# Planner of the RWKV recurrence stage: priority of the modulation rows, length of the small inverse's steps, gap before Tm's second group of matmuls

## Chip, cores and metric

The kernel runs on one NeuronCore of a Trainium2 chip. The metric is the device time of one execution in microseconds (us), the median of several runs. Engines are named as in the profile: PE (matmuls), DVE (vector engine), ACT (scalar engine), POOL (GpSimd, here almost only an issuer of DMAs) and SP (issuer of DMAs). Every engine works through its own queue in order, and waits for other engines through semaphores.

## The reference

One decoder block over 512 tokens with 2048 channels, all in float32. `c` gives six modulation vectors (shift, scale and gate for two sub-layers). The first sub-layer projects the modulated, RMS-normalised input once and feeds two mixers: RWKV-7 (a recurrence with a 64 x 64 state for each of 16 heads) and causal pooling. The second is a gated MLP.

```python
mod = silu(c) @ w_ada + b_ada                       # 6 * 2048
h = rmsnorm(x, g1) * (1 + sc1) + sh1
p = h @ w_in                                        # r, k, v, three small ranks, pool inputs
def step(S, inp):                                   # the recurrence, over 512 tokens
    sa = einsum('bhvk,bhk->bhv', S, a_t)
    S = S * w_t + sa * b_t + v_t * k_t
    y = einsum('bhvk,bhk->bhv', S, r_t)
y_pool[g] = (causal mean of u over (2, 4, 8, 16)[g] - u) @ pool_w[g]
x = x + gt1 * (concat(y_rwkv, y_pool) @ w_out)
h = rmsnorm(x, g2) * (1 + sc2) + sh2
x = x + gt2 * ((silu(gate) * val) @ w_down)         # gate, val: causal conv of h @ w_up
```

## The kernel before

The kernel has five stages in a row: the first eight column tiles of the input projection; the **recurrence stage**, which holds the other 27 column tiles beside the recurrence; the output projection; the up-projection; the down-projection. Only the recurrence stage is touched by the change.

In the recurrence stage activations lie channel by token, 128 x 512. Every float32 product is made of three fp32r matmuls (high and low halves, line 547), so the 27 tiles of `projection` are 27 x 48 = 1296 matmuls of 512 columns. Their weights come in 108 blocks: `weights` lets ACT round a block to its high half (516) and DVE subtract the low half (523), and ACT issues a later block's load. A block feeds 12 matmuls. The heads are worked off in eight pairs. For each pair `stage_a` makes decays and keys, scores, and the inverse of eight 64 x 64 unit triangular matrices; `stage_b` does the state. The inverse starts with 16 x 16 blocks: POOL carries them through DRAM into a layout with one block to a partition (lines 755, 759), DVE solves 14 steps of one multiply (769) and one add (771) each, in place (`xyl`), and POOL carries the result back (777, 781). `stage_b` then joins 16 to 32: 32 small matmuls into `pT` (886), a masked copy on DVE into `Tm` (890), 48 more matmuls which read `Tm` (896, 900), additions on DVE (903, 906); next 32 to 64 (914 to 933), the solves (940, 952 to 959), and a scan over the eight chunks in which six PE matmuls (980) alternate with six DVE steps (982). `post` normalises and gates the pair's output (1002 to 1023), and POOL stores it (1026).

Beside this, `ada_rows` makes three of the six modulation vectors, which are wanted only after the stage: 48 x 4 = 192 **modulation rows**, each a 256 KB load on SP (640) into one of five buffers and one DVE instruction with a sum (658) over it; four quarters, each with its own part `cq` of the activated `c` (635), which has one buffer.

The order of all this is not written out. Each chain is a Python generator that yields its next operation: engine, length, earliest time. `run` keeps a clock for each engine, and always takes the operation that can start first; on one engine it prefers one with a smaller priority number if that could start within 0.3 us of the first. The instructions are recorded in the order taken, and the chip keeps that order on each engine. The lengths are constants in the code; nothing at run time corrects them. Priorities: opening and evictions 0, `all_b` 1, `all_a` 2, weights 0 to 4 by how far ahead they are, `stage_k` 3, pool groups 5, projection 6, modulation rows 7. Row n is due from 3.0 + n * SPAN / 192 on, which is one row every 2.4 of the planner's microseconds; SPAN is 460 and a row's planned length ADAB is 0.72.

Of the kernel before, what the change touches and what calls it, by code (L numbers as in the profile page):

```python
# [9 lines left out]
F32 = mybir.dt.float32  # L10
# [6 lines left out]
P = 128  # L17
# [12 lines left out]
NA = 4  # L30
# [5 lines left out]
SPAN = 460.0  # L36
# [29 lines left out]
def block_kernel(ctx, tc, a, out, stop=None, dbg=None):  # L66
    nc = tc.nc
    V, S, G, PE = nc.vector, nc.scalar, nc.gpsimd, nc.tensor
# [126 lines left out]
    free_at = {"P": 0.0, "V": 0.0, "S": 0.0, "Q": 0.0, "G": 0.0}  # L195

    def spawn(prio, gen):
        chains.append([prio, gen, next(gen)])
# [188 lines left out]
    ra = actx.enter_context(tc.tile_pool(name="ra", bufs=1))  # L387
# [46 lines left out]
    def jl(j):  # L434
        return slice(j * L, (j + 1) * L)

    def rktile(name):
        return ra.tile([P, T], F32, tag="rk", name=name, bufs=3)

    def vtile(name):  # L440
        return ra.tile([P, T], F32, tag="v", name=name, bufs=2)

    def rpad(name):
        return ra.tile([P, 16 + T], F32, tag="rpad", name=name, bufs=4)
# [11 lines left out]
    modq = ra.tile([P, NA, 48], F32, tag="modq", name="modq")  # L456

    def load_lw(p):
        qs[p].lw = ra.tile([P, P], F32, tag="lw", name="lw")
        nc.sync.dma_start(qs[p].lw, a["lora"][p, :, 0, :])  # L460

    def load_pw(gi):
# [86 lines left out]
                cur[0] += 1  # L549
            spawn(0, evict(ti, ps, tag, t))  # L550

    upads = {}

    def evict(ti, ps, tag, t):
        if ti < 21:
            p, i = ti // 3 + 1, ti % 3
            q = qs[p]
            dst = vtile("v") if i == 2 else rktile("rk")
            t = yield "S", 0.6, t
            shift1(ps, 8 * i + p, dst)  # L560
            t = yield "V", 0.65, t
            shift2(ps, 8 * i + p, dst)
            mm.give(tag, t)
            if i == 0:
                q.rk = []
            if i < 2:
                q.rk.append((dst, t))
            else:
                q.v, q.made = (dst, t), t
        else:  # L570
            n, i = divmod(ti - 21, 2)
            gi = (1, 2, 0)[n]
            u = rpad("upad")
            V.memset(u[:, 0:16], 0.0)
            t = yield "S", 0.5, t
            S.copy(u[:, 16:], ps)
            mm.give(tag, t)
            if i == 0:
                upads[gi] = [load_pw(gi), u]
            elif gi:  # L580
                spawn(5, pool_group(gi, upads[gi][0], [upads[gi][1], u], t))
            else:
                upads[gi].append(u)

    def pool_front(gi, upad, t):
        win = WINS[gi]
        zs = []
        for i in range(2):
            cur_, lo, step = upad[i], 1, 1
            while step < win:  # L590
                t = yield "V", 0.64, t
                nxt = rpad("sw")
                V.tensor_add(nxt[:, lo:], cur_[:, lo:], cur_[:, lo - step : 16 + T - step])
                cur_ = nxt
                step *= 2
                lo += step
            z = upad[i][:, 16:]
            t = yield "V", 1.0, t
            edge = ra.tile([P, 16], F32, tag="edge", name="edge")
            V.tensor_mul(edge[:, 0:win], cur_[:, 16 : 16 + win], prec[:, 0:win])  # L600
            V.tensor_sub(edge[:, 0:win], edge[:, 0:win], z[:, 0:win])
            V.scalar_tensor_tensor(z, cur_[:, 16:], 1.0 / win, z, op0=ALU.mult, op1=ALU.subtract)
            V.tensor_copy(z[:, 0:win], edge[:, 0:win])
            zs.append(z)
        return zs, t
# [17 lines left out]

    def pool_group(gi, pw, upad, t):
        zs, t = yield from pool_front(gi, upad, t)
        yield from pool_back(gi, zs, pw, t + 2.0)

    last_mix = []
# [9 lines left out]
    def load_ada(n):  # L638
        t = ra.tile([P, AT], F32, tag="war", name="war", bufs=WARB)
        nc.sync.dma_start(t, a["ada2"][n // 48, n % 48, :, :])  # L640
        was.append(t)

    def ada_rows():
        n_all = 48 * NA
        step = SPAN / n_all
        t = yield "Q", 0.35, 1.0
        load_cq(0)
        tcq = t + 5.0
        land = {}
        for n in range(WARB - 1):  # L650
            t = yield "Q", 0.35, 0.0
            load_ada(n)
            land[n] = t + 6.0
        for n in range(n_all):
            kq, j = divmod(n, 48)
            t = yield "V", ADAB, max(land[n], tcq, 3.0 + n * step)
            wa = was.pop(0)
            V.scalar_tensor_tensor(wa, wa, 1.0, cqs[kq], op0=ALU.mult, op1=ALU.mult, accum_out=modq[:, kq, j : j + 1])
            if j == 47 and kq < NA - 1:
                tq = yield "Q", 0.35, t  # L660
                load_cq(kq + 1)
                tcq = tq + 5.0
            if n + WARB - 1 < n_all:
                tq = yield "Q", 0.35, 0.0
                load_ada(n + WARB - 1)
                land[n + WARB - 1] = tq + 6.0

    def stage_a(p, q):
        yield "-", 0.0, have(q, "made")
        (r, tr), (k, tk), (v, tv) = q.rk[0], q.rk[1], q.v  # L670
        lw = q.lw
# [91 lines left out]
        prod = ra.tile([64, 56], F32, tag="prod", name="prod")  # L763
        for s in range(1, 15):
            n = 15 - s
            t = yield "V", 0.36, t
            pv = prod[:, 0 : s * n].rearrange("p (j t) -> p j t", j=s)
            yv = xyl[:, 1, 0:s, s + 1 : 16]
            V.tensor_tensor(pv, xyl[:, 1, 0:s, s : s + 1].to_broadcast([64, s, n]),
                            nl[:, s : s + 1, s + 1 : 16].to_broadcast([64, s, n]), op=ALU.mult)  # L770
            V.tensor_add(yv, yv, pv)
            t -= 0.2
# [12 lines left out]
    def stage_k(p, q, t):  # L785
        (r, tr), (k, tk), (v, tv) = q.rk[0], q.rk[1], q.v
        al, em = q.al, q.em
        t = yield "S", 0.72, t
        S.activation(al, al, AF.Identity, bias=drv[:, 27 + p : 28 + p], scale=col("ka", p))
        t = yield "V", 0.63, t  # L790
        V.tensor_mul(k, k, al)
        kt = q.kt = ra.tile([P, T], F32, tag="kt", name="kt", bufs=2)
        t1 = yield "V", 0.63, t
        V.tensor_mul(ch(kt), ch(k), em[:, :, 1 : L + 1])
        q.tkt = t1
        t = yield "V", 0.68, t
        V.scalar_tensor_tensor(k, r, col("rk", p), k, op0=ALU.mult, op1=ALU.mult)
        t = yield "P", 1.1, pa.when(t)
        psb, tag = pa.take()
        PE.matmul(psb, bones, k, start=True, stop=True)  # L800
        bv = q.bv = ra.tile([P, T], F32, tag="bv", name="bv", bufs=2)
        t = yield "V", 0.63, t
        V.tensor_mul(bv, psb, v)
        pa.give(tag, t)
# [14 lines left out]
    def stage_b(p, q):  # L819
# [69 lines left out]
        t = yield "V", 0.36, t  # L889
        V.tensor_mul(Tm, r32(pT), mlev[:, None, :].to_broadcast([P, 8, 32]))  # L890
        pa.give(tag, t)
        t = yield "P", 1.0, max(t, tpb)
        pX = btile()[:, 0, :]
        for s in range(8):
            for b in range(4):
# [132 lines left out]
    def all_a():  # L1028
        for p in range(NP):
            yield from stage_a(p, qs[p])  # L1030

    def all_b():
        for p in range(NP):
            yield from stage_b(p, qs[p])
# [13 lines left out]
    pa.free.clear()  # L1048

    with tc.manual_schedule():  # L1050
        for prio, gen in ((0, opening()), (1, all_b()), (2, all_a()), (weights_prio, weights()), (6, projection()), (7, ada_rows())):
            spawn(prio, gen)
        run()

# [618 lines left out]
```

## Time and profile before

| | us |
|---|---|
| median of 3 runs | 2265.96 |
| lowest, highest | 2261.97, 2266.63 |
| profiled execution, its own time | 2266.95 |
| its span, first to last instruction | 2264.8 |
| lines 547, first to last (recurrence stage) | 140.6 to 688.1 |

The profile is of one execution. Times inside it are counted from the start of the span. "Idle before, releaser" is the time for which an engine stood still before an instruction, and what ended it. PEclk is the TensorE clock that the chip granted, 1.00 being full speed. A wait is put down to the dependency that came last.

### The profile page before, as it was taken

The numbers are of one execution on the slowest core, as the hardware profiler recorded it, in microseconds if no ns is written. First come the engines' busy times: TensorE is split into PE (matmuls) and PEld (weight loads), VectorE is DVE, ScalarE is ACT, GpSimd is POOL, SyncE is SP. The second block draws the span as 40 slices with busy tenths as digits, with TensorE's granted clock in tenths as the row PEclk, the third lists the DMA queues.
The fourth block names the chain that finished last, engine by engine and source line by source line (L and its number), as shares of the span: only waits on it lengthen the run. The fifth ranks groups of instructions, "written<-read, shape, count | busy, mean of one in ns | idle before, by whom it ended". The sixth has DMA issues, their size and how long they took to land.

```text
span 2264.8 us, 42575 instructions
## 1 busy us (share of the span) xinstructions
PE 2178.5 (96%) x17060; PEld 1908.8 (84%) x17060; DVE 1622.9 (72%) x2546; ACT 1019.7 (45%) x1465; POOL 217.8 (10%) x352
## 2 busy tenths in 40 slices
PE   6899989999999999999999999999999999999997
PEld 3666767677677889999999999999999888888886
DVE  7998878888764578888888877777777455353465
ACT  4353434343334356555555555555556322233453
POOL 0011111111010001100100000000000000110000
PEclk9999999999999999999999999999999999999999
DMA  9946566655537665988888877777777577663464
GB/s 395 374 165 188 174 186 181 174 159 149 176 113 248 190 196 186 287 239 244 234 237 245 220 199 198 194 196 203 198 198 218 180 264 262 209 205 114 131 191 155
DMA packets 169992, 468.64 MB, mean 207 GB/s; under 512 B 21361, under 2 KB 29505, under 8 KB 161729
## 3 DMA queue, kind: packets, MB, share of 16 engines
q1 hardware_dynamic: 128866, 364.45, 48.1%
q0 software_dynamic: 24752, 72.91, 15.5%
q10 hardware_dynamic: 16176, 28.58, 4.6%
q8 instruction: 133, 2.18, 0.4%
q14 instruction: 65, 0.53, 0.1%
HBM read 433.86 MB, written 31.99 MB: 206 GB/s over the span
## 4 chain that ended last, share of the span: by engine, by line
PE 70%; DVE 2%; DMA 1%; ACT 1%; issue 0%; DVEq 0%; ACTq 0%
PE b L133 18%; PE b L131 18%; PE b L132 18%; PE b L1110 5%; PE b L1111 3%; PE mm L547 2%; PE pa L612 0%; DMA wrow<-wup 0%; ACT x L1193 0%; DMA wraw<-wout 0%; PE mm L132 0%; PE mm L133 0%; PE py L133 0%; PE pa L133 0%; PE pa L132 0%
## 5 line engine op out<-in xcount | busy, mean ns | idle before, releaser
L133 PE MATMUL b<-t,ulo 128*128 128x256 f32 x1408 | 397.2, 282 | 0.0
L131 PE MATMUL b<-t,uhi 128*128 128x256 f32 x1408 | 396.8, 282 | 0.0
L132 PE MATMUL b<-t,uhi 128*128 128x256 f32 x1408 | 396.7, 282 | 0.0
L131 PE MATMUL b<-y,uhi 128*128 128x256 f32 x1056 | 298.2, 282 | 1.3 <-ACT uhi L1260 1.3
L133 PE MATMUL b<-y,ulo 128*128 128x256 f32 x1056 | 297.9, 282 | 0.3 <-DVE ulo L1262 0.3
L132 PE MATMUL b<-y,uhi 128*128 128x256 f32 x1056 | 297.8, 282 | 0.0
L547 PE MATMUL mm<-ahl,whi 128*128 128x512 f32 x864 | 294.5, 411 | 0.0
L1262 DVE TENSOR_TENSOR ulo<-wd,uhi 128x1024 fp32r<-128x1024 f32 (+1 forms) x120 | 136.0, 1134 | 207.7 <-ACT uhi L1260 198.7
L131 PEld LDWEIGHTS b<-t,uhi 128*128 128x128 f32 x1408 | 266.9, 190 | 0.0
L133 PEld LDWEIGHTS b<-t,ulo 128*128 128x128 f32 x1408 | 266.9, 190 | 0.0
L132 PEld LDWEIGHTS b<-t,uhi 128*128 128x128 f32 x1408 | 266.8, 190 | 0.0
L1260 ACT CAST uhi<-wquart 128x1024 fp32r<-128x1024 f32 x156 | 163.8, 1050 | 203.8 <-PE b L132 178.6
L1260 ACT CAST uhi<-wd 128x1024 fp32r<-128x1024 f32 (+1 forms) x120 | 117.3, 978 | 282.3 <-PE b L132 231.2
L1262 DVE TENSOR_TENSOR ulo<-wquart,uhi 128x1024 fp32r<-128x1024 f32 x156 | 190.7, 1223 | 71.4 <-ACT uhi L1260 71.3
L1260 ACT CAST uhi<-r 128x1024 fp32r<-128x1024 f32 x132 | 138.6, 1050 | 163.3 <-PE b L132 158.5
L133 PE MATMUL b<-act,ulo 128*128 128x512 f32 x528 | 208.7, 395 | 0.0
L131 PE MATMUL b<-act,uhi 128*128 128x512 f32 x528 | 208.1, 394 | 0.0
L132 PE MATMUL b<-act,uhi 128*128 128x512 f32 x528 | 208.1, 394 | 0.0
L1262 DVE TENSOR_TENSOR ulo<-r,uhi 128x1024 fp32r<-128x1024 f32 x132 | 161.2, 1221 | 62.6 <-ACT uhi L1260 62.6
L131 PEld LDWEIGHTS b<-y,uhi 128*128 128x128 f32 x1056 | 200.3, 190 | 1.8 <-ACT uhi L1260 1.7
L133 PEld LDWEIGHTS b<-y,ulo 128*128 128x128 f32 x1056 | 200.1, 190 | 0.7 <-DVE ulo L1262 0.7
L132 PEld LDWEIGHTS b<-y,uhi 128*128 128x128 f32 x1056 | 199.9, 189 | 0.1
(312 smaller groups left out, 4310.7 us busy)
## 6 DMA issues: line engine op xcount, KB each, us to landing
wquart<-wup SPq DMA_DIRECT2D x176, 512.0 KB, 4.8
wa<-ada SPq DMA_DIRECT2D x48, 1024.0 KB, 6.8
war<-ada SPq DMA_DIRECT2D x192, 256.0 KB, 4.5
wd<-wdn SPq DMA_DIRECT2D x80, 512.0 KB, 4.1
wraw<-win ACTq DMA_DIRECT2D x105, 256.0 KB, 4.1
wraw<-wout SPq DMA_DIRECT2D x96, 256.0 KB, 3.6
wquart<-wup POOLq DMA_DIRECT2D x44, 512.0 KB, 7.4
r<-wup SPq DMA_DIRECT2D x44, 512.0 KB, 4.5
```

The costliest lines, as they stand in the source:

```text
L131: PE.matmul(ps, wh, xh, start=start, stop=False, skip_group_check=more)
L132: PE.matmul(ps, wh, xl, start=False, stop=False, skip_group_check=more)
L133: return PE.matmul(ps, wl, xh, start=False, stop=stop, skip_group_check=more)
L547: PE.matmul(ps, w[:, sl], x, start=first, stop=k == KT - 1 and i == 2)
L1110: PE.matmul(ps[:, :].rearrange("p (a b) -> p a b", a=2), wh, x, start=start, stop=False)
L1111: PE.matmul(ps[:, 0:HT], wl, x[:, 0, :], start=False, stop=stop)
L1260: S.copy(hi[:, 0:n], src)
L1262: lo_of[0] = V.tensor_tensor(lo[:, 0:n], src, hi[:, 0:n].bitcast(F32), op=ALU.subtract)
```

## The change

All of it is in the planner's rules for the recurrence stage.

- **Rows.** The fixed priority 7 of `ada_rows` becomes `rows_prio`: 0 while DVE's planned clock is past the due time of the row three after the next one, else 7. A quarter's `cq` is taken to land 7 instead of 5 after its issue.
- **Small inverse.** A step (one multiply and one add) is planned at 0.46 instead of 0.36; the next one may still start 0.2 earlier.
- **Gap.** The second group of matmuls of the 16-to-32 join (896) may be planned no earlier than 3.0 after `Tm`.
- **Buffers.** The evictions of r and k wait, in the plan, for one of the three `rk` buffers (`rk_free`); before, only the chip waited. The loads `lw` get a second buffer. The copies of pool inputs wait for the pool group before (`pooling`).

No computing instruction is added or removed on any engine.

```diff
--- before.py
+++ after.py
@@ -434,7 +434,15 @@
     def jl(j):
         return slice(j * L, (j + 1) * L)
 
+    rk_made, rk_left = [0], []
+
+    def rk_free(t):
+
+        n = rk_made[0] - 3
+        return t if n < 0 else max(t, rk_left[n]) if n < len(rk_left) else None
+
     def rktile(name):
+        rk_made[0] += 1
         return ra.tile([P, T], F32, tag="rk", name=name, bufs=3)
 
     def vtile(name):
@@ -456,7 +464,7 @@
     modq = ra.tile([P, NA, 48], F32, tag="modq", name="modq")
 
     def load_lw(p):
-        qs[p].lw = ra.tile([P, P], F32, tag="lw", name="lw")
+        qs[p].lw = ra.tile([P, P], F32, tag="lw", name="lw", bufs=2)
         nc.sync.dma_start(qs[p].lw, a["lora"][p, :, 0, :])
 
     def load_pw(gi):
@@ -549,14 +557,14 @@
                 cur[0] += 1
             spawn(0, evict(ti, ps, tag, t))
 
-    upads = {}
+    upads, pooling = {}, [0.0]
 
     def evict(ti, ps, tag, t):
         if ti < 21:
             p, i = ti // 3 + 1, ti % 3
             q = qs[p]
+            t = yield "S", 0.6, t if i == 2 else (lambda t=t: rk_free(t))
             dst = vtile("v") if i == 2 else rktile("rk")
-            t = yield "S", 0.6, t
             shift1(ps, 8 * i + p, dst)
             t = yield "V", 0.65, t
             shift2(ps, 8 * i + p, dst)
@@ -570,14 +578,15 @@
         else:
             n, i = divmod(ti - 21, 2)
             gi = (1, 2, 0)[n]
+            t = yield "S", 0.5, (lambda t=t: None if pooling[0] is None else max(t, pooling[0]))
             u = rpad("upad")
             V.memset(u[:, 0:16], 0.0)
-            t = yield "S", 0.5, t
             S.copy(u[:, 16:], ps)
             mm.give(tag, t)
             if i == 0:
                 upads[gi] = [load_pw(gi), u]
             elif gi:
+                pooling[0] = None
                 spawn(5, pool_group(gi, upads[gi][0], [upads[gi][1], u], t))
             else:
                 upads[gi].append(u)
@@ -623,6 +632,7 @@
 
     def pool_group(gi, pw, upad, t):
         zs, t = yield from pool_front(gi, upad, t)
+        pooling[0] = t
         yield from pool_back(gi, zs, pw, t + 2.0)
 
     last_mix = []
@@ -639,13 +649,18 @@
         t = ra.tile([P, AT], F32, tag="war", name="war", bufs=WARB)
         nc.sync.dma_start(t, a["ada2"][n // 48, n % 48, :, :])
         was.append(t)
+
+    done_rows = [0]
+
+    def rows_prio():
+        return 0 if free_at["V"] > 3.0 + (done_rows[0] + 3) * SPAN / (48 * NA) else 7
 
     def ada_rows():
         n_all = 48 * NA
         step = SPAN / n_all
         t = yield "Q", 0.35, 1.0
         load_cq(0)
-        tcq = t + 5.0
+        tcq = t + 7.0
         land = {}
         for n in range(WARB - 1):
             t = yield "Q", 0.35, 0.0
@@ -654,12 +669,13 @@
         for n in range(n_all):
             kq, j = divmod(n, 48)
             t = yield "V", ADAB, max(land[n], tcq, 3.0 + n * step)
+            done_rows[0] = n + 1
             wa = was.pop(0)
             V.scalar_tensor_tensor(wa, wa, 1.0, cqs[kq], op0=ALU.mult, op1=ALU.mult, accum_out=modq[:, kq, j : j + 1])
             if j == 47 and kq < NA - 1:
                 tq = yield "Q", 0.35, t
                 load_cq(kq + 1)
-                tcq = tq + 5.0
+                tcq = tq + 7.0
             if n + WARB - 1 < n_all:
                 tq = yield "Q", 0.35, 0.0
                 load_ada(n + WARB - 1)
@@ -763,7 +779,7 @@
         prod = ra.tile([64, 56], F32, tag="prod", name="prod")
         for s in range(1, 15):
             n = 15 - s
-            t = yield "V", 0.36, t
+            t = yield "V", 0.46, t
             pv = prod[:, 0 : s * n].rearrange("p (j t) -> p j t", j=s)
             yv = xyl[:, 1, 0:s, s + 1 : 16]
             V.tensor_tensor(pv, xyl[:, 1, 0:s, s : s + 1].to_broadcast([64, s, n]),
@@ -798,6 +814,7 @@
         t = yield "P", 1.1, pa.when(t)
         psb, tag = pa.take()
         PE.matmul(psb, bones, k, start=True, stop=True)
+        rk_left.extend((t, t))
         bv = q.bv = ra.tile([P, T], F32, tag="bv", name="bv", bufs=2)
         t = yield "V", 0.63, t
         V.tensor_mul(bv, psb, v)
@@ -889,7 +906,7 @@
         t = yield "V", 0.36, t
         V.tensor_mul(Tm, r32(pT), mlev[:, None, :].to_broadcast([P, 8, 32]))
         pa.give(tag, t)
-        t = yield "P", 1.0, max(t, tpb)
+        t = yield "P", 1.0, max(t, tpb) + 3.0
         pX = btile()[:, 0, :]
         for s in range(8):
             for b in range(4):
@@ -1048,7 +1065,7 @@
     pa.free.clear()
 
     with tc.manual_schedule():
-        for prio, gen in ((0, opening()), (1, all_b()), (2, all_a()), (weights_prio, weights()), (6, projection()), (7, ada_rows())):
+        for prio, gen in ((0, opening()), (1, all_b()), (2, all_a()), (weights_prio, weights()), (6, projection()), (rows_prio, ada_rows())):
             spawn(prio, gen)
         run()
 
```

The lists that follow are instructions in the order recorded for one engine. In the new kernel lines after 434 have higher numbers: 523 is 531, 547 is 555, 658 is 674, 769 and 771 are 785 and 787, 886 is 903, 890 is 907, 896 is 913, 900 is 917, 982 is 999.

**PE, third head pair, between the two groups of the 16-to-32 join.** `x` holds the 16 x 16 inverses, `sb` the score matrices, `mm` the projection. Before:

```order
L886 MATMUL pa<-x_2713,sb 32x32 x32
L547 MATMUL mm<-ahl,whi 128x512
L547 MATMUL mm<-ahl,wlo 128x512
L547 MATMUL mm<-ahl,whi 128x512 x2
L547 MATMUL mm<-ahl,wlo 128x512
L547 MATMUL mm<-ahl,whi 128x512
L896 MATMUL pb<-x_2713,Tm_3164 32x32 x32
L900 MATMUL pb<-Tm_3164,x_2713 32x32 x16
```

With the change:

```order
L903 MATMUL pa<-x_2881,sb 32x32 x32
L726 MATMUL pa<-sq,hmat 128x512
L555 MATMUL mm<-ahl,wlo 128x512
L555 MATMUL mm<-ahl,whi 128x512 x2
L555 MATMUL mm<-ahl,wlo 128x512
L555 MATMUL mm<-ahl,whi 128x512 x2
L555 MATMUL mm<-ahl,wlo 128x512
L555 MATMUL mm<-ahl,whi 128x512 x2
L555 MATMUL mm<-ahl,wlo 128x512
L555 MATMUL mm<-ahl,whi 128x512 x2
L913 MATMUL pb<-x_2881,Tm_3359 32x32 x32
L917 MATMUL pb<-Tm_3359,x_2881 32x32 x16
```

Between the groups stood 6 projection matmuls; now 12, and the key norm's matmul of the next pair (line 726, formerly 710).

**DVE, third head pair, ahead of the copy into Tm.** `war` are modulation rows, `wlo` low halves of weight blocks, `cs` the decay sums of the next pair. Before:

```order
L658 SCALAR_TENSOR_TENSOR war,modq<-war,cq 128x512 x4
L450 SCALAR_TENSOR_TENSOR rk<-mm,vec,rk 128x511
L523 TENSOR_TENSOR wlo<-wraw,whi 128x512
L658 SCALAR_TENSOR_TENSOR war,modq<-war,cq 128x512 x2
L523 TENSOR_TENSOR wlo<-wraw,whi 128x512
L658 SCALAR_TENSOR_TENSOR war,modq<-war,cq 128x512 x4
L523 TENSOR_TENSOR wlo<-wraw,whi 128x512
L658 SCALAR_TENSOR_TENSOR war,modq<-war,cq 128x512 x2
L523 TENSOR_TENSOR wlo<-wraw,whi 128x512
L658 SCALAR_TENSOR_TENSOR war,modq<-war,cq 128x512 x2
L450 SCALAR_TENSOR_TENSOR v<-mm,vec,v 128x511
L890 TENSOR_TENSOR Tm_3164<-pa,mlev 128x256
```

With the change:

```order
L674 SCALAR_TENSOR_TENSOR war,modq<-war,cq 128x512 x5
L531 TENSOR_TENSOR wlo<-wraw,whi 128x512
L674 SCALAR_TENSOR_TENSOR war,modq<-war,cq 128x512
L531 TENSOR_TENSOR wlo<-wraw,whi 128x512
L674 SCALAR_TENSOR_TENSOR war,modq<-war,cq 128x512
L712 SCALAR_TENSOR_TENSOR cs<-scanm,sg 128x520
L716 COPY mid<-cs 128x8
L717 TENSOR_TENSOR cs<-cs,mid 128x520
L674 SCALAR_TENSOR_TENSOR war,modq<-war,cq 128x512
L531 TENSOR_TENSOR wlo<-wraw,whi 128x512
L907 TENSOR_TENSOR Tm_3359<-pa,mlev 128x256
```

Rows in runs of two and four, up to the copy, became rows that mostly stand alone; a run of five is left further up. Over the whole stage 36 rows stood alone on DVE and the longest run was seven; now 141 stand alone and the longest run is five.

**DVE, the scan of the third head pair.** `rw` is the state that the scan runs through, `xyl` and `prod` the small inverse of the pair after it. Before:

```order
L982 SCALAR_TENSOR_TENSOR rw<-pb,fdec,rw 128x64
L726 TENSOR_TENSOR bt<-sq,al 128x512
L982 SCALAR_TENSOR_TENSOR rw<-pb,fdec,rw 128x64
L728 TENSOR_TENSOR bt<-bt,em 128x512
L982 SCALAR_TENSOR_TENSOR rw<-pb,fdec,rw 128x64
L735 SCALAR_TENSOR_TENSOR ar<-sq,ep 128x512
L982 SCALAR_TENSOR_TENSOR rw<-pb,fdec,rw 128x64
L450 SCALAR_TENSOR_TENSOR rk<-mm,vec,rk 128x511
L982 SCALAR_TENSOR_TENSOR rw<-pb,fdec,rw 128x64
L737 TENSOR_TENSOR ar<-rk,ep 128x512
L982 SCALAR_TENSOR_TENSOR rw<-pb,fdec,rw 128x64
```

With the change:

```order
L999 SCALAR_TENSOR_TENSOR rw<-pb,fdec,rw 128x64
L778 TENSOR_TENSOR xyl<-nl,lanei 64x256
L785 TENSOR_TENSOR prod<-xyl,nl 64x14
L787 TENSOR_TENSOR xyl<-xyl,prod 64x14
L999 SCALAR_TENSOR_TENSOR rw<-pb,fdec,rw 128x64
L674 SCALAR_TENSOR_TENSOR war,modq<-war,cq 128x512
L999 SCALAR_TENSOR_TENSOR rw<-pb,fdec,rw 128x64
L785 TENSOR_TENSOR prod<-xyl,nl 64x26
L787 TENSOR_TENSOR xyl<-xyl,prod 64x2x13
L785 TENSOR_TENSOR prod<-xyl,nl 64x36
L787 TENSOR_TENSOR xyl<-xyl,prod 64x3x12
L999 SCALAR_TENSOR_TENSOR rw<-pb,fdec,rw 128x64
```

Between scan steps stood preparations of the next pair; now these stand ahead of the scan, and single rows and the small inverse of the next pair, from its first instruction on (778, formerly 762), stand there. So it is in the scans of the first and of the third to the seventh pair. On PE the stage's pairs end later: behind the last pair's last matmul (1012, now 1029) stood 73 of the 1296 projection matmuls, and now 15.

## The prediction

> **What bounds the kernel now.** I began with the busy time by stage, in five stretches that cover the recurrence stage. The columns are PE, PEld, DVE, ACT and POOL busy (instructions), the granted clock, DMA share and GB/s.
>
> ```profile
> 140.00:260.00 120.00, 111.95 (x1103) 84.26 (x1101) 101.46 (x259) 52.49 (x84) 22.84 (x42) 0.97 0.62 184
> 260.00:380.00 120.00, 111.59 (x1446) 85.85 (x1447) 99.61 (x260) 46.01 (x76) 21.69 (x40) 0.96 0.57 169
> 380.00:500.00 120.00, 112.62 (x1462) 85.69 (x1461) 98.68 (x255) 48.70 (x79) 18.36 (x34) 0.97 0.57 165
> 500.00:640.00 140.00, 129.19 (x1525) 97.15 (x1527) 111.23 (x294) 51.66 (x85) 25.05 (x47) 0.94 0.58 168
> 640.00:700.00 60.00, 59.95 (x599) 46.56 (x589) 33.94 (x71) 22.53 (x39) 2.17 (x4) 1.00 0.42 124
> ```
>
> PE sets the pace: it is busy for 525.3 of 560 us, and stands for 34.7. DVE is the second engine (444.9 of 560, 79%). The clock is below 1.00 in four of the five rows; that matters further down. The stage can gain no more than PE's idle time, plus what the reduced clock cost. So the next view is who PE waited for in the stage (us in total, times, longest).
>
> ```profile
> PE pb L896 <- DVE Tm L890: 16.6, 6, 4.9
> PE mm L547 <- DVE wlo L523: 6.2, 3, 4.2
> ```
>
> Half of PE's idle time is one wait, that of the join's second group for the copy into `Tm`, in six of eight pairs. The same view for DVE shows why so short a copy is late:
>
> ```profile
> DVE war L658 <- DMA war<-ada: 33.9, 34, 2.5
> DVE war L658 <- DMA cq<-cact: 5.2, 2, 2.6
> ```
>
> DVE stood for 39.1 us in front of modulation rows whose data had not landed, and what is behind them in its queue waits too. The third pair in the timeline, PE first, then DVE (start, length, what, idle before it and releaser):
>
> ```profile
> 315.04 0.75 PE L886 MATMUL pa<-x,sb 32*32 32x32 f32 x64
> ...
> 322.23 1.08 PE L896 MATMUL pb<-x,Tm 32*32 32x32 f32 x64 [4.85 <-DVE Tm L890]
> 323.11 1.05 PE L900 MATMUL pb<-Tm,x 32*32 32x32 f32 x32
> 324.08 1.22 PE L679 MATMUL pa<-xwa,lw 64*128 64x512 f32 x1
> ```
> ```profile
> 320.49 0.69 DVE L658 SCALAR_TENSOR_TENSOR war<-war,cq 128x512 f32<-128x512 f32 x1 [1.09 <-DMA war<-ada]
> ...
> 321.76 0.41 DVE L890 TENSOR_TENSOR Tm<-pa,mlev 128x256 f32<-128x256 f32 x1
> ```
>
> The first group ended at 315.79; the copy began at 321.76, behind a pile of rows, the last of which waited 1.09 us for its load. Six projection matmuls were too little cover.
>
> The reduced clock belongs to these gaps. These are the only stretches of the stage in which the clock was halved:
>
> ```profile
> 189.00:195.80 6.80, 4.50 (x11) 3.53 (x12) 6.29 (x19) 0.62 (x1) 2.44 (x5) 0.50 0.46 106
> 322.10:332.40 10.30, 10.17 (x145) 6.55 (x145) 5.80 (x14) 4.17 (x7) 0.00 (x0) 0.50 0.43 143
> 445.00:451.80 6.80, 4.95 (x102) 2.79 (x102) 4.26 (x12) 1.90 (x2) 0.00 (x0) 0.50 0.60 187
> 513.30:520.10 6.80, 5.02 (x104) 4.28 (x105) 6.12 (x14) 1.67 (x3) 0.00 (x0) 0.50 0.54 177
> 574.70:585.00 10.30, 9.70 (x143) 6.53 (x143) 5.66 (x15) 3.74 (x7) 0.00 (x0) 0.50 0.54 164
> ```
>
> Each begins at the end of one of the five longest PE gaps. Four are waits for `Tm`, the one above among them; the first is the wait for a weight block at 191.30, quoted below. Shorter gaps had no such effect: from 258 to 300 the clock stayed at 1.00 although PE stood for 1.59 us.
>
> ```profile
> 258.00:300.00 42.00, 38.10 (x584) 28.81 (x584) 36.87 (x97) 19.53 (x32) 4.72 (x9) 1.00 0.51 151
> 260.56 1.07 PE L886 MATMUL pa<-x,sb 32*32 32x32 f32 x64 [1.59 <-issue]
> ```
>
> **The change, part by part.** No instruction comes or goes, so the sum consists of waits alone. It is made against the profiled execution, 2266.95, which is 1.0 above the median.
>
> **Rows and gap: the wait for Tm, -16.** Now 12 or more projection matmuls stand between the groups in seven pairs, eight in the last, instead of 0 to 6. Two of them take 0.46 us, from start to start:
>
> ```profile
> 309.96 0.61 PE L547 MATMUL mm<-ahl,whi 128*128 128x512 f32 x2
> 310.42 0.39 PE L547 MATMUL mm<-ahl,wlo 128*128 128x512 f32 x1
> ```
>
> So 12 cover 2.8 us. That alone would leave part of the long waits, for the copy came 6.0 us after the first group in the example. But its lateness was the pile of rows, and with rows standing alone the four loads in flight have some 2.4 us of plan time for each row. Ahead of the copy remain about a row, a weight block and the copy, 0.69 + 0.69 + 0.41 = 1.8 us, under 2.8. Bounds: 16.6 if all goes, about 8 if the gap helps and the pile does not thin; I take 16. The longer gap costs nothing as long as projection matmuls fill it. Without that cover it is 3.0 us in eight pairs, 24 us; the recorded order has matmuls there in every pair.
>
> **Small inverse at its measured length: the wait for weight blocks, -4.** The 4.2 us of the second row of PE's waits fall into the first pair:
>
> ```profile
> 181.72 0.69 DVE L523 TENSOR_TENSOR wlo<-wraw,whi 128x512 fp32r<-128x512 f32 x1
> ...
> 190.57 1.88 DVE L523 TENSOR_TENSOR wlo<-wraw,whi 128x512 fp32r<-128x512 f32 x3
> 191.30 0.79 PE L547 MATMUL mm<-ahl,wlo 128*128 128x512 f32 x1 [4.24 <-DVE wlo L523]
> 185.19 0.20 DVE L769 TENSOR_TENSOR prod<-xyl,nl 64x44 f32<-64x44 f32 x1
> 185.65 0.21 DVE L769 TENSOR_TENSOR prod<-xyl,nl 64x50 f32<-64x50 f32 x1
> ```
>
> A step takes 0.46 us (185.19 to 185.65), and the plan of 0.36 loses 1.4 us over 14 steps. DVE made no low half for 8.9 us and PE ran dry. In the new order 14 blocks stand ahead of this inverse on DVE instead of 11, which is 36 matmuls or 8.2 us more cover. Bounds 0 and 6.2; I take 4, since the two other waits (2.0 in sum) have other places.
>
> **The clock, -13.** Take away the five long gaps and the halved stretches should go with them. In these PE was busy for 34.3 us (the five rows added up). From the start of 896 to what follows 900, the third pair took 322.23 to 324.08, 1.85 us; the fourth, at full clock, 1.17:
>
> ```profile
> 389.14 0.72 PE L896 MATMUL pb<-x,Tm 32*32 32x32 f32 x62 [0.59 <-DVE Tm L890]
> ...
> 390.31 0.73 PE L547 MATMUL mm<-ahl,whi 128*128 128x512 f32 x2
> ```
>
> At that ratio, 1.58, the 34.3 us would have been 21.7, a gain of 12.6; were all work twice as slow, 17.2. I take 13, near the measured ratio. [...]
>
> **What the new order costs, +8.** First the scan, +3. In six scans the small inverse's first instruction (762) now stands between scan steps. If its data (`nl`, which POOL carries through DRAM) is late, DVE holds up the scan, and PE's next 980 behind it. The data was there 11.2 us after the masked scores (746) in one pair and 14.6 in another:
>
> ```profile
> 349.83 1.28 DVE L746 TENSOR_TENSOR sb<-pa,masks 128x512 f32<-128x512 f32 x2
> 362.32 0.42 DVE L762 TENSOR_TENSOR xyl<-nl,lanei 64x256 f32<-64x256 f32 x1 [0.19 <-DMA nl<-dn]
> 472.07 1.28 DVE L746 TENSOR_TENSOR sb<-pa,masks 128x512 f32<-128x512 f32 x2
> 487.92 0.42 DVE L762 TENSOR_TENSOR xyl<-nl,lanei 64x256 f32<-64x256 f32 x1 [3.55 <-DMA nl<-dn]
> ```
>
> Bounds 0 and 6 x 3.55 = 21; of eight such steps two waited before, one of them long, so I take one or two long waits, less the 1 us of matmuls between scan steps: 3. Second the tail, +2: 15 projection matmuls (3.4 us) instead of 73 (16.6) follow the last pair's PE work, but the output projection needs that pair only at its end, and its first mixes now stand on DVE between the last scan steps; bounds 0 and 5. Third, +3 for waits that I cannot place: DVE does the same work in less time (444.9 in about 535, 83%). The second `lw` buffer, the later `cq` and the waits for `rk` and pools move waits that the plan did not know into it; PE's rows above show none of them, so they count 0.
>
> Sum: -16 - 4 - 13 + 3 + 2 + 3 = -25, and 2266.95 - 25 = **2242**.
>
> **Rivals.** **Late inverse stops the scans (slower).** The place is 762 between scan steps in six pairs. Before, it waited by 3.55 at most, once. From about 4 us on, PE's idle time there passes 3.0 (after 1 us of matmuls), the length of the shortest gap that had a halved clock; then each costs 3.1 of idle time and 13 / 5 = 2.6 of clock, six of them 34. Against the other terms (-28) that gives 2273. For it: POOL's descriptors share the DMA engines with rows now spread evenly. Against it: one long wait in eight, and 3.55 is short of 4. **The clock does not come back.** PE still halves, through several short gaps in a row or new long ones elsewhere: without the 13, 2255. For it: DVE at 83% with a strict order. Against it: the 258 to 300 row. [...] **The rows still pile up.** A run of five remains before the third pair's copy and others behind each change of quarter, so half of the `Tm` waits and of the clock stay: 2266.95 - 8 - 4 - 6 + 8 = 2257. For it: the 2.6 us wait for `cq`. Against it: 141 single rows. **All is given back** in small waits of scans: 2266, for which no row speaks in particular.
>
> **How the numbers follow.** Forecast 2242 with 0.62 (its own range 2232 to 2252); clock 0.12; rows 0.10; inverse 0.09; given back 0.07. A change is told from none from 0.2% on, 4.5 us, so faster is below 2261.4 and slower above 2270.5. The first three cases are faster: 0.84; same 0.07; slower 0.09. The range, 2229 to 2262, takes in the second and third case and, below, the clock at 17.2 and no cost from the new order (2266.95 - 16.6 - 6.2 - 17.2 + 2 = 2229).
>
> **What would show it.** Right: PE's wait for `Tm` under 2 us in all; DVE's wait for `war` under 15; a clock of 1.00 throughout the stage; the first output projection matmul near 663 instead of 688. Wrong: a wait of 980 for a scan step, or of DVE for `nl`, among PE's and DVE's largest; or halved stretches at new places.

## Result and the profile after

| | before | after |
|---|---|---|
| median of 4 runs each, us | 2265.86 | 2227.62 |
| lowest to highest | 2261.97 to 2266.63 | 2226.16 to 2228.68 |
| profiled execution, its span | 2266.95, 2264.8 | 2227.61, 2225.6 |
| recurrence stage, first to last projection matmul | 547.5 | 509.2 |
| PE idle in it | 34.5 | 9.0 |
| stretches of it at half the granted clock | 41.0 | 3.4 |

After stands to before as 0.9829, with a 95% interval of 0.981 to 0.9848. The gain is 38 us where 25 were forecast, and the time lies 1.4 us below the forecast range of 2229 to 2262. All but about 1 us of it falls in the recurrence stage, which became 38.3 us shorter: 25.5 us of PE's idle time, and 12.8 us by which PE's own work got shorter, as the halved clock went. (This split is good to about 1 us. PE's busy time depends a little on the order too: in e3 below, which has no halved stretch, it is 2.5 us less than in after, and the 3.4 us of half clock in after cannot account for all of that.)

The stage by stretches again, with the columns as before (PE, PEld, DVE, ACT and POOL busy, granted clock, DMA share, GB/s):

```profile
140.00:250.00 110.00, 109.31 (x1021) 84.09 (x1020) 99.33 (x259) 51.15 (x82) 16.72 (x31) 1.00 0.66 201
250.00:370.00 120.00, 119.02 (x1530) 90.93 (x1532) 103.59 (x271) 49.87 (x83) 23.87 (x44) 1.00 0.66 187
370.00:490.00 120.00, 116.91 (x1542) 89.32 (x1538) 104.54 (x276) 51.21 (x84) 23.36 (x44) 1.00 0.64 191
490.00:600.00 110.00, 109.06 (x1455) 84.15 (x1455) 96.46 (x258) 44.44 (x75) 19.39 (x37) 1.00 0.60 171
600.00:662.00 62.00, 58.53 (x577) 42.94 (x575) 34.80 (x75) 22.81 (x39) 6.36 (x12) 0.97 0.39 111
```

PE is busy for 512.8 of 522 us, and the clock is below 1.00 only in the last row. DVE has 438.7 us of work in these 522, 84%: it became no lighter, it became punctual. The waits of PE, in the same view as before (us in total, times, longest), have no `Tm` left:

```profile
PE pa L621 <- ACT mxp L625: 1.9, 1, 1.9
PE pa L903 <- issue: 1.5, 1, 1.5
PE mm L555 <- DVE rk L458: 1.4, 1, 1.4
...
PE mm L555 <- DVE wlo L531: 0.2, 1, 0.2
```

(The new line numbers are listed with the change.) The waits of DVE tell why:

```profile
DVE war L674 <- DMA war<-ada: 12.1, 12, 3.3
DVE Tm L907 <- PE pa L903: 7.5, 6, 2.0
```

DVE waits for a row's load 12 times, not 34, and the copy into `Tm` turned round: DVE now waits for PE's first group in six pairs, where PE waited for the copy in six. In the third pair's timeline (start, length, what, idle before) the copy follows the first group at once, and the second group comes 3.3 us after the end of the copy, with no idle time on PE:

```profile
325.51 0.75 PE L903 MATMUL pa<-x,sb 32*32 32x32 f32 x64
...
330.01 0.72 PE L913 MATMUL pb<-x,Tm 32*32 32x32 f32 x62
```
```profile
324.99 0.69 DVE L531 TENSOR_TENSOR wlo<-wraw,whi 128x512 fp32r<-128x512 f32 x1
...
326.31 0.42 DVE L907 TENSOR_TENSOR Tm<-pa,mlev 128x256 f32<-128x256 f32 x1 [0.63 <-PE pa L903]
```

The end of the stage: the first output projection matmul (131) follows the last one of the input projection without a gap, at 649.56 instead of 688.

```profile
649.33 0.39 PE L555 MATMUL mm<-ahl,wlo 128*128 128x512 f32 x1
649.56 0.39 PE L131 MATMUL pb<-ahl,whi 128*128 128x512 f32 x1
```

### The profile page after: what moved, and what is told of

It reads as the page before. It is cut to its first block, busy times and chain, and to the rows that moved or that the text cites. A ratio compares the mean times of both kernels' runs of the same rounds, so it can differ in the third digit from the quotient of the medians.

```text
span 2225.6 us, 42522 instructions
## 1 busy us (share of the span) xinstructions
PE 2164.2 (97%) x17060; PEld 1899.1 (85%) x17060; DVE 1617.2 (73%) x2546; ACT 1017.6 (46%) x1465; POOL 218.0 (10%) x352
## 3 DMA queue, kind: packets, MB, share of 16 engines
q0 software_dynamic: 24752, 72.91, 15.6%
## 4 chain that ended last, share of the span: by engine, by line
PE 85%; DVE 9%; DMA 2%; issue 2%; ACT 2%; POOL 0%; DVEq 0%; ACTq 0%; SPq 0%; POOLq 0%
PE b L133 18%; PE b L132 18%; PE b L131 18%; PE mm L555 11%; PE b L1127 6%; DVE wa L289 3%; PE b L1128 3%; PE pb L957 1%; DVE war L674 1%; DVE wlo L328 1%; PE pa L621 0%; DMA wraw<-win 0%; DMA wrow<-wup 0%; PE pb L997 0%; POOL x L797 0%
## 5 line engine op out<-in xcount | busy, mean ns | idle before, releaser
L555 PE MATMUL mm<-ahl,whi 128*128 128x512 f32 x864 | 290.0, 409 | 2.0 <-DVE rk L458 1.4
## 6 DMA issues: line engine op xcount, KB each, us to landing
wquart<-wup SPq DMA_DIRECT2D x176, 512.0 KB, 4.9
wd<-wdn SPq DMA_DIRECT2D x80, 512.0 KB, 4.1
wquart<-wup POOLq DMA_DIRECT2D x44, 512.0 KB, 7.3
r<-wup SPq DMA_DIRECT2D x44, 512.0 KB, 4.4
```

Source lines behind the costliest of these rows:

```text
L555: PE.matmul(ps, w[:, sl], x, start=first, stop=k == KT - 1 and i == 2)
```

## Experiments

Three questions were open: which part of the change carries the gain, why the new order cost nothing, and what idle time halves the clock. Each kernel is after (in e6, before) with the edit shown. "Stage", "idle" and "halved" are measured as in the table above, in the one profiled execution of each; the ratio is to runs of before on the same chip, with its 95% interval. Before had medians of 2264.64 to 2267.78 beside them, so that differences of 2 or 3 us between runs that do not stand side by side say little. The profiled executions of e1 (2254.03) and e5 (2238.47) are the slowest of their four, so their stage, idle and halved are rather high.

| | median | ratio | interval | stage | idle | halved |
|---|---|---|---|---|---|---|
| e1 rows undone | 2249.57 | 0.9916 | 0.9899 to 0.9932 | 533.5 | 24.6 | 23.9 |
| e2 gap 0 | 2235.94 | 0.9858 | 0.9843 to 0.9872 | 516.2 | 15.8 | 6.8 |
| e3 step 0.36 | 2229.43 | 0.9828 | 0.9814 to 0.9843 | 509.8 | 12.1 | 0 |
| e4 buffers alone | 2268.06 | 0.9996 | 0.9978 to 1.0014 | 550.3 | 35.7 | 44.4 |
| e5 rows and buffers | 2233.95 | 0.9852 | 0.9835 to 0.9869 | 520.0 | 15.6 | 13.7 |
| e6 before, gap alone | 2253.53 | 0.9935 | 0.9918 to 0.9951 | 534.6 | 25.0 | 17.1 |
| e7 long gaps | 2292.97 | 1.011 | 1.0095 to 1.0125 | 571.9 | 57.4 | 64.9 |
| e8 gap 2.0 | 2233.19 | 0.9849 | 0.9834 to 0.9864 | 514.4 | 14.3 | 6.8 |
| e9 short gaps | 2258.36 | 0.9966 | 0.9947 to 0.9984 | 537.7 | 27.5 | 27.3 |
| e10 late `nl` | 2229.02 | 0.984 | 0.9812 to 0.9868 | 507.9 | 7.9 | 3.4 |
| e11 no gap in the last pair | 2229.87 | 0.9846 | 0.9818 to 0.9873 | 510.0 | 10.5 | 3.4 |
| e12 gap 4.0 | 2232.0 | 0.9858 | 0.9825 to 0.9892 | 512.0 | 11.6 | 6.8 |

### Which part carries the gain

**e1, the rows undone.** Fixed priority, `cq` again taken to land after 5.0; gap, step and buffers stay.

```diff
-        tcq = t + 7.0
+        tcq = t + 5.0
-        for prio, gen in (... (6, projection()), (rows_prio, ada_rows())):
+        for prio, gen in (... (6, projection()), (7, ada_rows())):
```

> The changed kernel with the modulation rows back at priority 7 and the quarter's vector at 5; gap, step length and buffer waits as changed. Theory rows (the pile of rows made Tm late): the pile is back, 12 matmuls cover 2.8 us of it, of the old latenesses (6.0, 4.9, 4.6, 3.7 us) some 7 us of PE waits for Tm remain, and one or two halved stretches: 2238 to 2246. Rival gap (the cover alone removed the wait): 2227 to 2231, no wait for Tm over 1 us in all.

About 20 us of the gain are lost (22 by the medians, 20 by the ratios), half of it or a little more; the time is 4 us above the range expected for this case. PE's second group hardly waits for the copy into `Tm` (0.9 us, where 7 were expected), since the gap covers it. But DVE is late again, and it shows elsewhere: at the next join (931), at a weight block, and at 696, the next pair's first matmul, which needs the PSUM tile that the late copy reads:

```profile
PE pb L931 <- DVE x L923: 5.9, 3, 2.9
PE pa L696 <- DVE Tm L907: 5.2, 2, 3.7
PE mm L555 <- DVE wlo L531: 4.5, 1, 4.5
```

DVE waits for rows even longer than in before (33.9 us, 34 times), in the same view of DVE:

```profile
DVE war L674 <- DMA war<-ada: 40.9, 43, 5.0
```

So the pile of rows is a cause of its own, and whatever stands behind it pays; `Tm` was only the first in line.

**e2, e3, e4: gap, step, and nothing but the buffers.** e2 takes `+ 3.0` away, e3 plans a small inverse's step at 0.36; e4 undoes rows, step and gap together, so that only the buffer waits and the second `lw` buffer are left.

```diff
-        t = yield "P", 1.0, max(t, tpb) + 3.0
+        t = yield "P", 1.0, max(t, tpb)
```
```diff
-            t = yield "V", 0.46, t
+            t = yield "V", 0.36, t
```

> The changed kernel without the 3.0 before the second group. Theory rows: the copy into Tm starts at once, PE waits at most 0.6 us in each of eight pairs, no halved stretch by it: 2228 to 2233. Rival gap: waits for Tm of 10 us and more, halved stretches behind them: 2242 to 2255.

> The changed kernel with the small inverse's step planned at 0.36 again. Theory rows: DVE is 1.4 us behind its plan after each inverse, 0 to 1 us of PE waits a pair, perhaps the first pair's wait for a weight block: 2228 to 2234. Rival (the plan's length of the inverse is what keeps DVE on time): 2240 or more, with PE waits for weight blocks or scan steps over 8 us.

> Of the change only the planned waits for buffers and the second lw buffer; rows at 7, step 0.36, no gap. Theory rows: like the kernel before, 2260 to 2268, with the waits for Tm and the halved stretches back. Rival buffers (the plan that knows its buffers is what removed the small waits, the 8 us that I had charged): 2245 to 2257, PE's waits other than Tm and weight blocks down from 11.9 to under 9.5 us.

The buffers alone give nothing: 0.9996, with PE's largest wait as in before.

```profile
PE pb L913 <- DVE Tm L907: 16.2, 5, 6.5
PE mm L555 <- DVE wlo L531: 5.0, 3, 4.3
```

The step is worth nothing that could be told: 1.8 us by the medians, and by the ratios none. With 0.36 shorter waits for weight blocks appear (3.8 us in three), while the last halved stretch is gone. The long wait for a weight block in the first pair, 4.2 us in before, does not come back in e3. It does in e1, at the same place, although e1 plans the step at 0.46: it is the 4.5 us in e1's rows above. On DVE, 14 blocks stand ahead of the first pair's inverse in e3 as in after, and 11 in e1 as in before. So it is the rows' priority that moves these blocks forward, and not the step.

Without the gap 7 to 8 us are lost; the time lies between the two ranges expected. They are no wait for `Tm`, of which 1.3 us show up. The largest wait is at the pool group's matmul (621):

```profile
PE pa L621 <- DVE upad L612: 3.9, 1, 3.9
PE pb L997 <- DVE rw L999: 1.5, 1, 1.5
PE pb L913 <- DVE Tm L907: 1.3, 1, 1.3
```

**e5, rows and buffers without gap and step; e6, before with the gap alone.** Their edits are those above.

> Rows' priority, the later quarter vector and the buffer waits, which that order needs; step at 0.36 and gap 0 as before. If the parts add up (2227.6 + 8.3 for the gap + 1.8 for the step): 2235 to 2241, waits for Tm under 3 us. Rival (rows help only together with the gap): 2248 or more, waits for Tm over 8 us.

> The kernel before with nothing but the 3.0 before the second group. Theory rows: the pile stays, 12 matmuls hide 2.8 us of each of the six waits, so 8 to 13 of the 16.6 us and two or three of the four halved stretches go: 2248 to 2256. Rival gap (cover is enough): 2242 or less, waits for Tm under 2 us.

The rows, with the buffer waits, give 33 us alone; the gap gives 14 alone. Together they gave 38, so they overlap: each by itself cures most of the wait for `Tm`. In e5, 1 us faster than expected, 0.5 us of it are left. In e6 the second group no longer waits for it, but 680, which needs the PSUM tile, does for 4.4 us; DVE still waits for rows (36 times, 40.6 us), and PE stands for other things too:

```profile
PE mm L547 <- DVE wlo L523: 4.8, 2, 4.6
PE pa L680 <- DVE Tm L890: 4.4, 3, 1.9
PE pa L886 <- issue: 4.2, 2, 2.5
PE pa L886 <- DMA x<-dx: 3.4, 3, 1.7
```

In e5 the rows' loads hold DVE for 8.8 us. No run has the rows without the buffer waits. So the 33 us belong to both together; e4 shows only that the buffers alone give nothing.

**e8, e11, e12: other gaps.** 2.0, 4.0, and 3.0 in all pairs but the last, whose pool group waits in after.

```diff
-        t = yield "P", 1.0, max(t, tpb) + 3.0
+        t = yield "P", 1.0, max(t, tpb) + (3.0 if p < 7 else 0.0)
```

> The changed kernel with 2.0 in place of 3.0. Theory rows: the copy is on time, 8 matmuls cover it as well as 12, so 2226 to 2231. Rival (the gap's worth lies in which order the planner happens to find): anywhere from 2222 to 2238, with the difference in waits that have nothing to do with Tm.

> The changed kernel with the gap 3.0 in pairs one to seven and 0 in the last, where pool matmuls fill the place. If PE's waits of 1.5 and 1.9 us there, and the halved stretch behind them, come from the gap: 2222 to 2226. If from the pool group's buffers: 2226 to 2229.

> The changed kernel with 4.0 in place of 3.0. If the gap's worth is cover for Tm: 2226 to 2230, since 12 matmuls were enough. If it lies in which order the planner happens to find (0 gave 2235.9, 2.0 gave 2233.2, 3.0 gave 2227.6): anywhere from 2224 to 2238.

By gap the medians are 2235.9 (0), 2233.2 (2), 2227.6 (3) and 2232.0 (4): the sum of a few single waits that every new order deals out afresh, more than a matter of cover for `Tm`. The intervals of these runs overlap, so it is the waits in the profiles that tell them apart, and not the medians. The largest one is that of the pool group's matmul in the last pair, with 2.0 (below) and, at 3.8 us, with 4.0:

```profile
PE pa L621 <- ACT mxp L625: 3.9, 1, 3.9
```

e11 was to remove that wait. It did, and put another in its place, the copy of the pair that had lost its gap:

```profile
PE pb L913 <- DVE Tm L907: 3.6, 1, 3.6
```

At 2229.9, just above both ranges expected, it gained nothing over after. No version here beats after, and its 9.0 us of idle time are what is left to win in this stage without less work.

### Whether the small inverse's data is near to holding up the scan

**e10.** Seven small POOL instructions stand ahead of the load of `nl` in each pair, to make it land 3.8 us later.

```diff
+        for _ in range(7):
+            G.memset(x4, 0.0)
```

> The changed kernel with seven more clearings of x4 on POOL (0.55 us each, 3.8 us) ahead of the load of nl, so that the small inverse's data lands 3.8 us later in every pair, which the plan does not know. Theory (the plan holds 12.6 us for it, and it lands after 11.2, so the scans have 1.4 us to spare): DVE waits some 2.4 us for nl in five to seven pairs, and PE some 1.5 us in each scan: 2236 to 2246. Rival (matmuls between scan steps hide all of it): 2227 to 2231.

The delay did not come out as meant. POOL stands at this place anyway, until the transfers to DRAM before it have landed, and the seven instructions mostly fill that time. In the second pair POOL stood for 5.14 us in after (first line); in e10 the seven take 4.05 us of it, and the load is issued 0.4 us later:

```profile
230.69 0.55 POOL L775 DMA_DIRECT2D nl<-dn  x1 [5.14 <-DMA dn<-sb]
```
```profile
225.57 4.05 POOL L776 MEMSET x<- 128x512 f32 x7
231.11 0.55 POOL L777 DMA_DIRECT2D nl<-dn  x1 [1.50 <-DMA dn<-sb]
```

By the traces' records of landings, `nl` is there 0.4 to 2.1 us later after the masked scores than in after, and not 3.8. DVE waits for `nl` three times, at most 0.9 us (0.5 once, in after), and PE's waits have no scan step among them:

```profile
DVE xyl L780 <- DMA nl<-dn: 2.3, 3, 0.9
```

The median is 1.4 us above that of after, and the ratios overlap. So e10 answers its question for a small delay only. How much room there is can be read from after itself: in five pairs the data had landed 0.9 to 3.5 us before DVE came to 778, and in the other three at most 0.1 us before. Those three are the pairs that wait in e10. What a later landing does stands in e3, where DVE waited for 2.38 us within the scan of the first pair and held up the scan's next matmul on PE:

```profile
233.71 0.42 DVE L778 TENSOR_TENSOR xyl<-nl,lanei 64x256 f32<-64x256 f32 x1 [2.38 <-DMA nl<-dn]
```
```profile
234.78 0.43 PE L997 MATMUL pb<-rw,gd 128*128 128x64 f32 x2 [1.58 <-DVE rw L999]
```

### Which idle time halves the clock

**e7, e9: a ladder of gaps.** Multiplications on POOL behind the copy delay `Tm` by another amount in each pair; seven pairs are delayed, the last is not.

```diff
         V.tensor_mul(Tm, r32(pT), mlev[:, None, :].to_broadcast([P, 8, 32]))
+        for _ in range((7, 11, 8, 9, 10, 13, 15, 0)[p]):
+            G.tensor_tensor(Tm, Tm, mlev[:, None, :].to_broadcast([P, 8, 32]), op=ALU.mult)
```

In e9 the counts are 6, 6, 5, 4, 4, 5, 6, 0.

> The changed kernel with 7, 11, 8, 9, 10, 13, 15 and 0 repeats of the mask's multiplication on POOL after Tm (the mask is 0 or 1, so the values stay), about 0.62 us each, so that PE stands before the second group by about 1.0, 2.2, 1.7, 3.8, 2.9, 4.8, 5.8 and 0 us in pairs one to eight. Theory clock (a PE gap of 3 us or more halves the clock for 6.8 to 10.2 us and costs 2.6 us more): no halved stretch in pairs one to three, one each in pairs four, six and seven, perhaps five; 22 us of gaps and 8 to 10 of clock: 2256 to 2261. Rival (halved stretches have another cause): the clock stays 1.00 there, 2248 to 2252.

> The ladder with 6, 6, 5, 4, 4, 5, 6 and 0 repeats, which took 0.91 us each in the first ladder. Counted down from the gaps there, PE should stand by 3.3, 1.9, 2.4, 1.3, 1.3, 1.9, 2.3 and 0 us before the second group in pairs one to eight. Theory threshold (only gaps of 3 us halve the clock): one halved stretch, in pair one; 14 us of gaps and 2.5 of clock: 2242 to 2246. Rival (what counts is the share of PE's idle time in some fixed stretch, so that gaps of 1.5 to 2.5 us halve it too, now and then): two to five halved stretches, 2247 to 2256.

One multiplication took 0.91 us, and not the 0.62 that was the author's estimate (a quarter of the 2.34 us that POOL took over 128 x 1024 in before is 0.59), so that in e7 every gap was longer than planned, 4.2 to 10.5 us (and the time far above both ranges), and each was followed by 6.8 to 13.7 us at half clock. The stage is 62.7 us longer than in after, of which 48.4 are idle time and 14.3 the clock, 2.0 for a gap. e9 has the short ones. The seven gaps (idle time at the end of the row):

```profile
215.02 1.07 PE L915 MATMUL pb<-x,Tm 32*32 32x32 f32 x64 [3.44 <-POOL Tm L909]
277.95 0.72 PE L915 MATMUL pb<-x,Tm 32*32 32x32 f32 x62 [2.46 <-POOL Tm L909]
343.70 0.81 PE L915 MATMUL pb<-x,Tm 32*32 32x32 f32 x63 [3.08 <-POOL Tm L909]
402.10 1.02 PE L915 MATMUL pb<-x,Tm 32*32 32x32 f32 x64 [2.69 <-POOL Tm L909]
464.90 0.72 PE L915 MATMUL pb<-x,Tm 32*32 32x32 f32 x62 [1.64 <-POOL Tm L909]
524.30 0.72 PE L915 MATMUL pb<-x,Tm 32*32 32x32 f32 x62 [2.75 <-POOL Tm L909]
587.28 1.08 PE L915 MATMUL pb<-x,Tm 32*32 32x32 f32 x64 [3.29 <-POOL Tm L909]
```

and the clock behind each of them (columns as in the stretches above; the clock is the third number from the right):

```profile
214.50:221.30 6.80, 6.28 (x131) 4.99 (x133) 2.54 (x5) 0.00 (x0) 0.93 (x2) 0.50 0.13 48
279.40:282.80 3.40, 3.40 (x14) 2.17 (x15) 2.44 (x6) 0.63 (x1) 0.00 (x0) 0.51 0.06 18
344.20:347.60 3.40, 3.40 (x67) 2.85 (x55) 2.10 (x5) 0.00 (x0) 0.00 (x0) 0.50 0.00 0
402.20:405.60 3.40, 3.40 (x100) 3.04 (x100) 2.04 (x5) 0.00 (x0) 0.31 (x1) 0.50 0.66 222
462.00:470.00 8.00, 6.36 (x147) 4.91 (x146) 6.85 (x13) 2.48 (x5) 3.16 (x4) 1.00 0.31 102
525.10:528.50 3.40, 3.40 (x34) 2.76 (x29) 2.45 (x5) 0.00 (x0) 0.00 (x0) 0.50 0.02 5
586.50:593.30 6.80, 6.02 (x121) 4.73 (x123) 2.54 (x5) 0.00 (x0) 1.19 (x2) 0.50 0.01 3
```

Gaps of 2.46 to 3.08 us are followed by one halved stretch of 3.4 us, those of 3.29 and 3.44 by two in a row; after 1.64 the clock stays. That is six gaps with a halved stretch where the rival expected two to five, and the time is 2 us above its range. The bound of 3.0 is refuted. But no other length of a gap is the bound either: e5 has a gap of 1.57 us that was followed by a halved stretch (first line), and e6 one of 2.55 that was not (second line).

```profile
378.89 1.07 PE L903 MATMUL pa<-x,sb 32*32 32x32 f32 x64 [1.57 <-issue]
```
```profile
261.10 1.21 PE L886 MATMUL pa<-x,sb 32*32 32x32 f32 x64 [2.55 <-issue]
```

What counts is where a gap falls. Within a run, the halved stretches start whole multiples of 3.413 us apart: in before, those at 322.1, 445.0, 513.3 and 574.7 start 39, 75, 95 and 113 such lengths after the one at 189.0, and each of the five lasts two or three such lengths (6.83 and 10.24 us). Time is thus cut into windows of 3.413 us in these traces, and the clock changed only at their borders. PE's idle time was counted in every such window from 150 to 710 us, in all fourteen profiles; what follows is about the windows that were themselves at full clock. All 32 windows with 1.87 us or more of idle time were followed by one at half clock. Of the 29 with 1.2 to 1.85 us, 8 were. Of some 2170 with less, one was (0.74 us, in e6). The 1.57 us of e5 lie within one window; the border cuts the 2.55 us of e6 into 1.81 and 0.74, and the 1.64 of e9 into 0.40 and 1.23. What decides between 1.2 and 1.85 us stays open.

This also explains the one halved stretch of after, which comes behind two waits of the last pair:

```profile
610.99 1.07 PE L903 MATMUL pa<-x,sb 32*32 32x32 f32 x64 [1.52 <-issue]
...
616.01 2.62 PE L621 MATMUL pa<-upad,pw 128*128 128x512 f32 x4 [1.91 <-ACT mxp L625]
```
```profile
613.81:617.22 3.41, 1.50 (x5) 0.68 (x4) 3.24 (x8) 1.28 (x2) 0.56 (x1) 1.00 0.21 47
617.20:620.60 3.40, 3.40 (x99) 1.98 (x98) 0.17 (x2) 0.78 (x1) 0.54 (x1) 0.50 0.61 189
```

The 1.91 us fall into one window whole; the 1.52 lie ahead of it. The same two waits were followed by a halved stretch in e10, where the second again lies within one window, but not in e7 and e9, where a border divides it (in e9 into 0.69 and 1.25). So the two do not add up, and whether the second one halves the clock depends on where it falls. The least idle time from which on the next window was always halved, 1.87 us, is a little over half of a window.

## Why the prediction was right and wrong

**Wait for `Tm`, -16: right.** It went from 16.6 to 0, and by the mechanism given: the pile thinned out and the gap covers the rest. e5 and e6 show that either of the two would nearly have done for this wait. e1 and e6 show what the sum could not: with the pile left in place, its lateness moves on to other waits.

**Weight blocks, -4: 2 too small, and not for the reason given.** They went from 6.2 to 0.2. I kept back 2.0 for two waits elsewhere, and these went too. The long wait of the first pair was to go because the inverse's length is planned as measured. It went because of the rows: with them undone and the step at 0.46 it is there (e1, 4.5 us), with the rows and the step at 0.36 it is not (e3, e5). In before, five of the last six rows ahead of that inverse had kept DVE waiting, for 4.0 us in all. At most the shorter waits of e3 (3.8 us) and e5 (3.0 us) are the step's.

**Clock, -13: right, 12.8, with some luck.** The ratio of matmul groups at both clocks (1.58) gave the size. As 3.4 us of half clock stayed, the 12.8 came from 30.9 us of PE's work and not from 34.3, which is a ratio of 1.71. For three of the five stretches I had also misread the start: those at 189.0, 445.0 and 513.3 begin 1.8 to 2.3 us before the end of their gap, and not at it. The bound behind the term was wrong. I took 3.0 us as the gap from which the clock halves, because the shortest of the long gaps had 3.0 and one of 1.59 had no effect. What counts is idle time within one window of 3.413 us: after 1.87 us or more the next one was always halved (32 of 32), after 1.2 to 1.85 sometimes (8 of 29). "A clock of 1.00 throughout the stage" failed for that reason in one stretch of 3.4 us. It cost the sum little, since after has no single gap above 1.91.

**"What the new order costs", +8: this step failed.** It cost nothing, and PE's other waits even fell, from 11.7 (34.5 - 16.6 - 6.2) to 8.8 us (9.0 - 0.2), so the term measured -2.9. That is 11 of the 13 us by which the sum was off; the weight blocks are the other 2. Of its three parts:

- The scan, +3: 0. PE never waits at the scan for this inverse, and DVE waits 0.5 us for `nl`. I had the landing time from two pairs, 11.2 and 14.6 us after the masked scores, and took them as what any pair may do. The traces hold all eight: 9.6 to 15.0 us in before, 9.6 to 13.5 in after. How late the data lands does not decide alone: the latest, 15.0, cost no wait, because DVE came to it later still. The mechanism itself is real, and three pairs of after have at most 0.1 us of room; in e3 it cost PE 1.6 us, once.
- The tail, +2: 0. The output projection follows without a gap.
- "Waits that I cannot place", +3: -2.9. A busier DVE was to bring new ones. It did, in the pool group (1.9), `rk` (1.4) and the first group (1.5), but these are smaller than the old ones that went with the pile: 2.9 us for 847 on ACT's `rw` became 1.1, for one.

The range ended at 2229 because its lower bound still held 2 us for the new order. A thing that cannot be placed can go either way; with a gain of a few us allowed there, it would have held the result.

**The rivals.** "Late inverse stops the scans" is refuted for after by its own waits, which have no scan step among them. No run made the data as late as that rival asks (4 us of waiting); the nearest, within a scan, is e3 with 2.38. The page of after counts POOL's DMA queue (15.6%) and the one with the rows' loads (49.0%) against the same 16 DMA engines, but the data landed no later for it: 13.5 us behind the masked scores at most, where before had 15.0. "The clock does not come back" is refuted by the stretches, and e7 and e9 show what it would have cost. "The rows still pile up" is what e1 shows with the rows undone: 2249.6, where I had 2257 for half of it. "All is given back" did not come.

**The signs.** `Tm` under 2 us: 0. DVE's wait for `war` under 15: 12.1. First output projection matmul near 663: 649.6, as the gain was larger. One sign of being wrong came too, on a small scale: a halved stretch at a new place, 617.2.

## What to carry to other kernels

When an engine that works in order makes something that another one is waiting for, look at what stands ahead of it in its queue. Here 192 instructions that nobody needs before the end of the stage, each with a load of its own, held up whatever came behind them: in before DVE stood for 33.9 us in front of 34 of them. Lengthening the distance at one victim (e6) gave 14 us; spreading the 192 (e5, with the buffer waits) gave 33. Count waits of the pacing engine twice, once as idle time and once for the clock that they may take with them (25.5 and 12.8 us here). Do not credit a gain to the part of a change that was meant for it before a run without that part has been read: the first pair's wait went with the rows, and not with the step. And check in the trace that an added delay has arrived: the one of e10 was mostly hidden in time in which POOL stood anyway.

## What the hardware showed

- The clock was halved for whole windows of 3.413 us, whose borders lay on one grid within a run (in before the halved stretches start 39, 75, 95 and 113 windows after the first). After a window at full clock with 1.87 us or more of idle PE time the next one was halved (32 of 32); with 1.2 to 1.85 us it was in 8 of 29. A gap of 2.55 us that a border divided had no effect (e6), one of 1.57 within a window had it (e5).
- Halved stretches cost about a third of their length or less: 37.6 us of them cost 12.8 (before to after), 61.5 us more cost 14.3 (after to e7). PE was busy for 34.3 of their 41.0 us in before.
- POOL's multiplication of 128 x 256 float32 elements took 0.91 us in e7 (below), where DVE's copy with a mask over as many, read from PSUM, took 0.42 in after:

```profile
L909 POOL TENSOR_TENSOR Tm<-Tm,mlev 128x256 f32<-128x256 f32 x73 | 66.6, 912 | 60.1 <-DVE Tm L907 32.8 <-DVE mid L716 8.7 <-ACT whi L524 6.9
```
